# Hybrid encoder trunk on one core: down-projection steps between the last FFN products, low parts of the output weights on another engine, and a different choice of memory slots

## The chip, the cores and the metric

The kernel runs on one core of one Trainium2 chip. A core has a matrix engine (TensorE, "PE" in the profile, whose weight loads are listed as "PEld"), a vector engine (VectorE, "DVE"), a scalar engine (ScalarE, "ACT") and a general engine (GpSimd, "POOL"). Each works through its own queue in order. A fifth queue, SyncE ("SP"), issues the transfers between the chip's main memory (DRAM) and the on-chip buffers (SBUF). TensorE writes its sums into PSUM. The metric is the device time of one execution in microseconds (us). Lower is better.

## The reference

A transformer-like encoder layer is applied to two batches that share their weights: a prompt of 512 rows and a sample of 1024 rows, both 1024 wide, in 32-bit floating point. For each batch:

```python
h = rmsnorm(x); z = h @ w_in            # 1024 -> 1792, columns: q, k, v, ca, cb
a = window_attention(q, k, v)           # 8 heads of 64, |q - k| <= 128, 2 kv heads,
                                        # T5 bias, one sink logit per head
c = ca * sigmoid(cb)
c = silu(layernorm(depthwise_conv31(c)))
x = x + concat(a, c) @ w_out            # 1024 -> 1024
h = rmsnorm(x)
u = depthwise_conv3(h @ w_up)           # 1024 -> 2 * 2816
x = x + (silu(u[:, :2816]) * u[:, 2816:]) @ w_down
y = rmsnorm(x)
```

Attention looks at blocks of 128 rows and their two neighbours. The outputs are y for the prompt and y for the sample.

## The kernel before

**Products in 32 bits.** Each operand of a product is split into a high part, rounded to the format that TensorE multiplies, and a low part, the rest. A product a x b is then three matmuls into the same PSUM sums: high x high, high x low, low x high. `split` (lines 199 to 204) does it for weights: ScalarE casts the high part (L202), and VectorE or GpSimd subtracts it from the raw tile to get the low part (L203), by its argument `dve`. In the same way L969 and L965 (`split_of`) make operands of the later stages, and L1407 those of the gate columns.

**Stages.** (1) The prompt's input projection. (2) The sample's input projection (L309, L310, L312 are the three matmuls of one projection step); a side queue puts the prompt's attention, output projection and second norm between its steps (`prompt()`). (3) The prompt's FFN up projection over 22 column blocks, `ffn_step(k)`; from k = 2 on, the side queue interleaves the sample's attention and the preparation of its output weights (`sample()`). (4) The sample's output projection (L736 to L738), with sums of the prompt's gated products between. (5) The sample's FFN over 22 column blocks j, with a scheme of seven products (`first` to `seventh`, in the code's order) in place of eight per two by two blocks. Each is twelve matmuls (L1089 to L1091). (6) The down projection of both batches, by the same seven-product scheme, with the order of the products 1, 2, 5, 6, 7, 4, 3. Each has eleven steps p over pairs of column blocks; step p has three groups w, six matmuls each (L1423 to L1425): w = 0 and 1 for the sample, w = 2 for the prompt. (7) Residual, final norm and stores.

**Attention and its norm.** Scores go through VectorE (L592), ScalarE's exponential (L610), VectorE's reciprocal (L614) and a scaling (L618 on ScalarE, L620 on GpSimd). `conv_norm` transposes a block (L700), takes statistics (L702, L703), has GpSimd compute the root (L186, L187), scales (L706) and transposes back (L712). Convolution taps run on VectorE (L364), with some offloaded to ScalarE and GpSimd (L356, L357).

**The prompt's FFN step.** `up_half` runs 24 matmuls into one of two PSUM banks named u. ScalarE makes the middle tap with the bias (L866), VectorE adds two taps (L862) and so frees the bank. `gate` multiplies the two halves (L886, L891, L892).

**The sample's output weights.** In `sample()` after attention, 16 tiles of 128 x 512 are loaded (`load_wo`, L761 and L763) and split. `m % 4 < DW2` chooses VectorE for the low part; `DW2` is 0, so all 16 are on GpSimd. The prompt's 16 (`DW` = 2, `kc % 2 < DW`) are all on VectorE.

**The last FFN pair.** At j = 21, the last column block, the loop runs second, sixth, the value part of block 20, (no first of a block 22), seventh, then the first step of the down projection (two groups), (no fifth), fourth, the gate part, third. Between the sixth and the seventh lies ScalarE's copy of a sum out of PSUM (L1172), between the seventh and the fourth another (L1181). The down projection's loads come through `load_next`, which takes the next tile from a list (`ahead`): activations `ga` and gate columns `gt` or `gb` that were stored to DRAM before, and `w_down`. `operands(i, p)` makes the high and low parts for a step; `make(k + lead)` does so `lead` steps ahead of use (4 as a rule, 1 for the first step).

**What sets the order.** The program is written as one sequence. A planner simulates the engines and orders each engine's queue by readiness and by place in the program, except where `manual_schedule` keeps the written order: from the sample's FFN on for PE, and from the down projection's first step on for SP and PE. There a second block is opened after the seventh product of j = 21.

**Slots.** SBUF tiles come from a list of named slots: 15 q (4096 bytes per partition), 4 c (4224), 61 h (2048), 2 d (2176) and 32 small ones. `Slots.tile` (lines 80 to 102) takes the first free one of the smallest size that fits; freed slots go to the end of the list. A tile in a slot must wait until the last reader of the slot's former tile is done. When no slot under 4096 bytes is left, a q slot is cut into two halves of 2048 (`Half`), as long as more than `KEEP` = 3 q slots are free.

Of the kernel before, what the change touches and what calls it, by code (L numbers as in the profile page):

```python
# [15 lines left out]
P = 128  # L16
# [12 lines left out]
NJ = FF // P  # L29
# [18 lines left out]
SCB, SCD = "aapa", "aaap"  # L48


WOP, WOA, DW, DW2 = 1, 5, 2, 0
NE = 2
YN = 2
OB = "uc"
# [4 lines left out]

BACK = (200, 1500)  # L60
U0 = 2


FILL = 216
# [2 lines left out]
class Slots:  # L67
# [3 lines left out]


    def __init__(self, pool, classes, halved=None, keep=0):
        self.pool, self.free, self.n = pool, [], 0
        self.halved, self.keep, self.halves = halved, keep, {F32: [], F32R: []}
        for kind, (count, size) in classes.items():
            for i in range(count):
                self.free.append((f"{kind}{i}", size))

    def tile(self, shape, dt=F32, nbytes=4, among=None):  # L80
        need = nbytes
        for s in shape:
            need *= s
        fits = [s for s in self.free if s[1] >= need and (among is None or s[0][0] in among)]
        if self.halved and nbytes == 4 and need <= 2048 and not any(s[1] < 4096 for s in fits):
            halves = self.halves[dt]
            if not halves and sum(s[0][0] == self.halved for s in fits) > self.keep:
                slot = next(s for s in fits if s[0][0] == self.halved)
                self.free.remove(slot)
                self.n += 1  # L90
                whole = Whole(self, slot, dt, (self.pool(slot[0]) if callable(self.pool) else self.pool).tile([P, 2, 512], dt, tag=slot[0], name=f"{slot[0]}_{self.n}", bufs=1))
                halves += [(whole, 0), (whole, 1)]
                whole = None
            if halves:
                return Half(*halves.pop(0), shape)
        if not fits:
            raise RuntimeError(f"no slot for {need} bytes")
        least = min(s[1] for s in fits)
        slot = next(s for s in fits if s[1] == least)
        self.free.remove(slot)  # L100
        self.n += 1
        return Held(self, slot, (self.pool(slot[0]) if callable(self.pool) else self.pool).tile([P] + list(shape), dt, tag=slot[0], name=f"{slot[0]}_{self.n}", bufs=1))


class Held:
# [4 lines left out]
        return self.t[i]  # L110

    def __del__(self):
        self.slots.free.append(self.slot)


class Whole:
# [6 lines left out]
class Half:  # L123
# [14 lines left out]
    def __del__(self):  # L138
        w = self.whole
        w.out -= 1  # L140
        if w.out:
            w.slots.halves[w.dt].append((w, self.i))
        else:
            w.slots.halves[w.dt] = [h for h in w.slots.halves[w.dt] if h[0] is not w]
            w.slots.free.append(w.slot)


@with_exitstack
def tile_hybrid_encoder(ctx: ExitStack, tc: tile.TileContext, xs, rel_bias, norm_attn_g, w_in,
# [151 lines left out]
    def drain(queue):  # L301
        while queue:
            advance(queue)
# [531 lines left out]
    drain(side)  # L835
    load_kv()
    drain(convs)


    def want_up(k, half):  # L840
# [494 lines left out]
    def load_next(n):  # L1335
        for _ in range(n):
            if ahead:
                key, p = ahead.popleft()
                roomy = sum(f[0][0] in "qc" for f in sb.free) > 5
                if (key, p) in second_half:  # L1340
                    t = second_half.pop((key, p))
                elif key in BRIEF and p % 2 == 0 and p + 1 < NPAIR and roomy:
                    both = sb.tile([2, NT])
                    t, second_half[key, p + 1] = Part(both, 0), Part(both, 1)
                    both = None
                else:
                    t = sb.tile([NT])
                pr[key, p] = t
                what, i, n2 = key
                if what == "a":  # L1350
                    src = ga[i, p][:]
                elif what == "g":
                    n = min(2, NPAIR - 2 * p)
                    for q in range(n):
                        j, h = {1: (0, HL), 2: (1, HL), 4: (1, HR)}.get(i, (0, None))
                        src = gb[i, 2 * p + q][:] if h is None else gt[2 * (2 * p + q) + j][:, h]
                        nc.sync.dma_start(t[:, q * HT:(q + 1) * HT], src)
                    continue
                else:
                    src = w_down[0, (2 * p + i) * P:(2 * p + i + 1) * P, n2 * NT:(n2 + 1) * NT]  # L1360
                nc.sync.dma_start(t[:], src)
# [146 lines left out]
    def group(i, p, w, lead=LEAD):  # L1508

        k = ORDER.index(i) * NPAIR + p  # L1510
        if len(pr) < CAP and sum(f[0][0] == "h" for f in sb.free) > ROOM:
            load_next(1)
        make(k + lead)
        if w not in pd:
            pd[w] = wide()
        for q in range(2):
            mm_down(pd[w][:, q * NT:(q + 1) * NT], i, p, 2 * w + q)
        left[i, p] = left.get((i, p), NW3) - 1
        if left[i, p] == 0:
            hl.pop((i, p))  # L1520
            if p % 2 == 1 or p == NPAIR - 1:
                hp.pop((i, p // 2))
        if p == NPAIR - 1:
            evacuate(i, w, pd.pop(w))

    def first_step():
        load_next(8)
        for w in range(2):
            group(1, 0, w, 1)

    def product(i):
        rest = [(p, w) for p in range(2, NPAIR - 2) for w in range(NW3)]
        if i == 1:
            order = [(1, 0), (1, 1), (0, 2), (1, 2)]
        else:
            order = [(p, w) for w in range(NW3) for p in range(2)]
        order += rest + [(p, w) for w in range(NW3) for p in (NPAIR - 2, NPAIR - 1)]
        for p, w in order:
            group(i, p, w)
            if w < NW3 - 1:  # L1540
                continue
            if i == 7 and p == 4:
                load_x1(0, 0)
# [127 lines left out]
```

## Time and profile before

| What | Value |
|---|---|
| time, median of 3 runs | 1543.17 us (1542.73 to 1548.15) |
| time of the profiled execution | 1547.91 us |
| its span, from the first to the last instruction | 1546.1 us |
| TensorE busy | 1491.7 us, 96% |
| VectorE busy | 1125.0 us, 73% |
| ScalarE busy | 795.3 us, 51% |
| GpSimd busy | 704.0 us, 46% |
| moved by DMA | 227.17 MB, 147 GB/s on average |

A row of groups reads: line, engine, operation, output <- inputs by the program's names (buffer numbers left out; q, h, c, d are slots in SBUF, u, a, b, c, w banks in PSUM by the place in which they stand, other names are tensors in DRAM), shape, count, then busy us, mean ns of one, and the idle time of the engine just before them with what ended it. A row of waits reads: engine and line that waited, what it waited for, us in total, times, longest. A row of the timeline begins with the start in us and the duration. In tables of stretches each row is one stretch of the span with the busy us of each engine. Busy matmuls overlap: the profile gives one of 128x512 some 389 ns, while the next one starts earlier.

### The profile page before, as it was taken

Reading aid. Unit: us, or ns where it says so; the run is one execution under the profiler, and the core shown is the slowest. Engines: PE = TensorE matmul, PEld = TensorE weight load, DVE = VectorE, ACT = ScalarE, POOL = GpSimd, SP = SyncE. Lnnn points to the kernel's source line nnn. Section 1 sums busy time; section 2 is a strip of 40 time slices with the busy share of each in tenths; the row PEclk is TensorE's granted clock in tenths of the full one; section 3 lists DMA queues with packets and bytes.
Section 4 is the critical chain, followed back from the end, with each engine's and each line's share of the span. In section 5 each row is a group of like instructions: output and inputs, shape, how many; then the busy total and the mean of one; then the engine's idle time right before and its main releaser. Section 6 shows DMA issues by size and latency. Waiting matters only on the chain.

```text
span 1546.1 us, 20081 instructions
## 1 busy us (share of the span) xinstructions
PE 1491.7 (96%) x6843; PEld 1228.5 (79%) x6843; DVE 1125.0 (73%) x1608; ACT 795.3 (51%) x1404; POOL 704.0 (46%) x562
## 2 busy tenths in 40 slices
PE   8999998899999999899999999999999899999998
PEld 6787787787888888777777888888888788888886
DVE  7998767857879795434677777777776855668885
ACT  4644654335777776713454544555445633343355
POOL 7652343225667766956423555555545000003345
PEclk9999999899999999999999999999999999999999
DMA  6572334447344435868422233333331582356654
GB/s 226 163 216 80 104 102 125 130 132 223 103 130 130 131 121 165 257 215 287 158 82 69 96 107 105 102 103 102 103 133 51 194 299 86 108 166 214 211 184 163
DMA packets 228780, 227.17 MB, mean 147 GB/s; under 512 B 13268, under 2 KB 168348, under 8 KB 228549
## 3 DMA queue, kind: packets, MB, share of 16 engines
q1 hardware_dynamic: 228677, 225.88, 45.4%
q8 instruction: 54, 0.88, 0.2%
q14 instruction: 49, 0.40, 0.1%
HBM read 164.74 MB, written 62.14 MB: 147 GB/s over the span
## 4 chain that ended last, share of the span: by engine, by line
PE 72%; DMA 4%; DVE 2%; POOL 2%; ACT 2%; issue 1%; SPq 1%; POOLq 0%; ACTq 0%; DVEq 0%
PE w L1091 8%; PE w L1090 8%; PE w L1089 8%; PE w L1423 7%; PE w L1424 7%; PE w L1425 7%; PE u L312 5%; PE u L309 5%; PE u L310 5%; PE u L736 1%; PE u L738 1%; PE u L737 1%; DMA h<-gt 1%; PE b L309 1%; PE b L310 1%
## 5 line engine op out<-in xcount | busy, mean ns | idle before, releaser
L203 POOL TENSOR_TENSOR q<-q,q 128x1024 fp32r<-128x1024 f32 x72 | 173.5, 2415 | 93.6 <-ACT q L202 37.6
L965 POOL TENSOR_TENSOR q<-q,q 128x512 fp32r<-128x512 f32 x101 | 140.7, 1399 | 157.9 <-ACT q L1075 145.8
L965 DVE TENSOR_TENSOR h<-h,h 128x512 fp32r<-128x512 f32 (+2 forms) x202 | 158.2, 816 | 63.1 <-ACT h L969 24.3
L1423 PE MATMUL w<-h,h 128*128 128x512 f32 x462 | 179.8, 389 | 0.6 <-ACT h L969 0.6
L1425 PE MATMUL w<-h,h 128*128 128x512 f32 x462 | 179.8, 389 | 0.0
L1424 PE MATMUL w<-h,h 128*128 128x512 f32 x462 | 179.7, 389 | 0.0
L1089 PE MATMUL w<-h,q 128*128 128x512 f32 x448 | 175.1, 391 | 3.9 <-ACT w L1181 2.2
L1091 PE MATMUL w<-h,q 128*128 128x512 f32 x448 | 174.5, 389 | 1.1 <-POOL q L965 1.1
L309 PE MATMUL u<-h,q 128*128 128x512 f32 x400 | 160.0, 400 | 7.7 <-DVE h L862 4.6
L1090 PE MATMUL w<-h,q 128*128 128x512 f32 x426 | 165.8, 389 | 0.0
L310 PE MATMUL u<-h,q 128*128 128x512 f32 x400 | 157.9, 395 | 0.0
L312 PE MATMUL u<-h,q 128*128 128x512 f32 x384 | 152.4, 397 | 1.3 <-POOL q L203 1.3
L364 DVE SCALAR_TENSOR_TENSOR c<-c,cvw,c 128x512 f32<-128x512 f32 x184 | 138.0, 750 | 2.9
L962 POOL TENSOR_TENSOR q<-q,q 128x1024 f32<-128x1024 f32 x12 | 32.8, 2742 | 235.6 <-DMA h<-gb 195.5
L969 ACT CAST h<-h 128x512 fp32r<-128x512 f32 x120 | 71.7, 620 | 96.7 <-DVE h L965 47.7
L309 PE MATMUL b<-h,q 128*128 128x512 f32 x256 | 102.8, 401 | 4.0 <-DVE d L394 2.9
L1089 PEld LDWEIGHTS w<-h,q 128*128 128x128 f32 x448 | 84.1, 188 | 22.5 <-ACT w L1181 2.6
L862 DVE SCALAR_TENSOR_TENSOR h<-u,fw,h 128x511 f32<-128x511 f32 x88 | 65.4, 743 | 50.3 <-ACT h L866 49.5
L1423 PEld LDWEIGHTS w<-h,h 128*128 128x128 f32 x462 | 86.7, 188 | 19.1 <-ACT h L969 1.0
L310 PE MATMUL b<-h,q 128*128 128x512 f32 x256 | 101.5, 396 | 0.0
L312 PE MATMUL b<-h,q 128*128 128x512 f32 x256 | 101.5, 396 | 0.0
L1425 PEld LDWEIGHTS w<-h,h 128*128 128x128 f32 x462 | 86.7, 188 | 18.1
(417 smaller groups left out, 3656.1 us busy)
## 6 DMA issues: line engine op xcount, KB each, us to landing
q<-in_w_up SPq DMA_DIRECT2D x88, 512.0 KB
ga<-q SPq DMA_DIRECT2D x64, 256.0 KB
h<-ga SPq DMA_DIRECT2D x57, 256.0 KB
q<-in_w_in SPq DMA_DIRECT2D x28, 512.0 KB
h<-in_w_down SPq DMA_DIRECT2D x52, 256.0 KB
q<-in_x_sample SPq DMA_DIRECT2D x15, 512.0 KB
h<-qsd SPq DMA_DIRECT2D x24, 256.0 KB
x1d<-q SPq DMA_DIRECT2D x11, 512.0 KB
```

Source lines behind the costliest of these rows:

```text
L203: (nc.vector if dve else nc.gpsimd).tensor_tensor(lo[:], raw[:], hi[:].bitcast(F32), op=ALU.subtract)
L309: nc.tensor.matmul(out, whi[:, kc, :], hi[:], start=(kc == 0), stop=False)
L310: nc.tensor.matmul(out, whi[:, kc, :], lo[:], start=False, stop=False)
L312: nc.tensor.matmul(out, wlo[:, kc, :], hi[:], start=False, stop=(kc == KC - 1))
L364: nc.vector.scalar_tensor_tensor(acc[:], src(t), w(t), acc[:], op0=ALU.mult, op1=ALU.add)
L965: (eng or nc.vector).tensor_tensor(out, a, b, op=ALU.subtract)
L1089: nc.tensor.matmul(out, whi[:, s], hi[:], start=(start and c == 0), stop=False, **go)
L1090: nc.tensor.matmul(out, whi[:, s], lo[:], start=False, stop=False, **go)
L1091: nc.tensor.matmul(out, wlo[:, s], hi[:], start=False, stop=(stop and c == 3), **go)
L1423: nc.tensor.matmul(out, sh[:, c], th[:], start=(p == 0), stop=False)
L1424: nc.tensor.matmul(out, sh[:, c], tl[:], start=False, stop=False)
L1425: nc.tensor.matmul(out, sl[:, c], th[:], start=False, stop=(p == NPAIR - 1))
```

## The change

Three things are changed.

1. In the last FFN pair (j = 21), the second block of hand-written order for SP and PE is opened before the seventh product instead of after it, and 18 tiles are loaded there in one go (before: 10 and then 8). Four steps p = 0 to 3 of the down projection's first product, with their groups w = 0 and 1, are put between the pair's products: two groups before the seventh, two between the seventh and the fourth, two between the fourth and the third, and two after the third. Before, two groups of step 0 stood there. Their operands are made one step ahead. `product(1)` then leaves out the groups already done.
2. `DW2` is 4 instead of 0: the low parts of all 16 tiles of the sample's output weights are subtracted on VectorE instead of GpSimd.
3. `Slots.tile` counts its calls as a clock and notes when each slot and each half became free. A free half is taken in place of a whole small slot when it has been free longer than the first small slot that fits. While `sb.old` is `OLD` = 24 (from the side queue's `prompt()` to the end of the sample's input projection), a q slot is also cut into halves when the small slot on offer has been free for fewer than 24 calls and the q slot for longer, if more than `KEEP` q slots are free. Otherwise `sb.old` is 0 and a q slot is cut only when no small slot fits, as before.

```diff
-WOP, WOA, DW, DW2 = 1, 5, 2, 0
+WOP, WOA, DW, DW2 = 1, 5, 2, 4
+OLD = 24
...
+    def give(self, slot):
+        self.since[slot[0]] = self.clock
+        self.free.append(slot)
+
+    def split_whole(self, slot, dt):
+        self.free.remove(slot)
+        self.n += 1
+        t = (...).tile([P, 2, 512], dt, tag=slot[0], name=f"{slot[0]}_{self.n}", bufs=1)
+        whole = Whole(self, slot, dt, t)
+        since = self.since.get(slot[0], -OLD)
+        self.halves[dt] += [(whole, 0, since), (whole, 1, since)]
+
     def tile(self, shape, dt=F32, nbytes=4, among=None):
+        self.clock += 1
...
-        if self.halved and nbytes == 4 and need <= 2048 and not any(s[1] < 4096 for s in fits):
+        least = min((s[1] for s in fits), default=0)
+        slot = next((s for s in fits if s[1] == least), None)
+        if self.halved and nbytes == 4 and need <= 2048:
             halves = self.halves[dt]
-            if not halves and sum(s[0][0] == self.halved for s in fits) > self.keep:
...
-            if halves:
-                return Half(*halves.pop(0), shape)
+            wholes = [s for s in fits if s[0][0] == self.halved]
+            since = self.since.get(slot[0], -OLD) if slot and slot[1] < 4096 else self.clock
+            if halves and (min(h[2] for h in halves) < since or since == self.clock):
+                return Half(*self.oldest(halves), shape)
+            if (since == self.clock or self.clock - since < self.old) and len(wholes) > self.keep and \
+                    self.since.get(wholes[0][0], -OLD) < since:
+                self.split_whole(wholes[0], dt)
+                return Half(*self.oldest(halves), shape)
...
     side.append(prompt())
+    sb.old = OLD
     pace.update(rate=RB, conv=CB, late=CL)
...
     drain(convs)
+    sb.old = 0
...
-    def first_step():
-        load_next(8)
-        for w in range(2):
-            group(1, 0, w, 1)
+    filled = set()
+
+    def fill(*which):
+        for p, w in which:
+            group(1, p, w, 1)
+            filled.add((p, w))
 
     def product(i):
         rest = [(p, w) for p in range(2, NPAIR - 2) for w in range(NW3)]
+        order = [(p, w) for w in range(NW3) for p in range(2)]
+        order += rest + [(p, w) for w in range(NW3) for p in (NPAIR - 2, NPAIR - 1)]
         if i == 1:
-            order = [(1, 0), (1, 1), (0, 2), (1, 2)]
-        else:
-            order = [(p, w) for w in range(NW3) for p in range(2)]
-        order += rest + [(p, w) for w in range(NW3) for p in (NPAIR - 2, NPAIR - 1)]
+            order = [g for g in order if g not in filled]
...
         value_part(j - 1)
+        last = j == NJ - 1
+        if last:
+            by_hand.__exit__(None, None, None)
+            by_hand = tc.manual_schedule(engines={mybir.EngineType.SP, mybir.EngineType.PE})
+            by_hand.__enter__()
+            load_next(18)
+            fill((0, 0), (1, 0))
         first(j + 1)
         split_up(j + 1, 6)
         seventh(j)
-        if j == NJ - 1:
-            by_hand.__exit__(None, None, None)
-            by_hand = tc.manual_schedule(engines={mybir.EngineType.SP, mybir.EngineType.PE})
-            by_hand.__enter__()
-            load_next(10)
-            first_step()
+        if last:
+            fill((0, 1), (1, 1))
         fifth(j + 1)
         split_up(j + 1, 7)
         fourth(j)
         gate_part(j)
         split_up(j + 1, 4)
+        if last:
+            fill((2, 0), (2, 1))
         third(j)
         split_up(j + 1, 3)
+    fill((3, 0), (3, 1))
```

More of the change, by code (lines that the diff above doesn't have):

```diff
@@ L73, in __init__ @@
     def __init__(self, pool, classes, halved=None, keep=0):
-        self.pool, self.free, self.n = pool, [], 0
+        self.pool, self.free, self.n, self.clock, self.since, self.old = pool, [], 0, 0, {}, 0
         self.halved, self.keep, self.halves = halved, keep, {F32: [], F32R: []}
@@ L78, in __init__ @@
                 self.free.append((f"{kind}{i}", size))
+    def give(self, slot):
[4 more added lines that the diff above has]
+        self.n += 1
+        t = (self.pool(slot[0]) if callable(self.pool) else self.pool).tile([P, 2, 512], dt, tag=slot[0], name=f"{slot[0]}_{self.n}", bufs=1)
+        whole = Whole(self, slot, dt, t)
+        since = self.since.get(slot[0], -OLD)
+        self.halves[dt] += [(whole, 0, since), (whole, 1, since)]
     def tile(self, shape, dt=F32, nbytes=4, among=None):
+        self.clock += 1
         need = nbytes
@@ L84, in tile @@
         fits = [s for s in self.free if s[1] >= need and (among is None or s[0][0] in among)]
-        if self.halved and nbytes == 4 and need <= 2048 and not any(s[1] < 4096 for s in fits):
+        least = min((s[1] for s in fits), default=0)
+        slot = next((s for s in fits if s[1] == least), None)
+        if self.halved and nbytes == 4 and need <= 2048:
             halves = self.halves[dt]
-            if not halves and sum(s[0][0] == self.halved for s in fits) > self.keep:
[L88 to L93, printed above, removed]
-            if halves:
-                return Half(*halves.pop(0), shape)
-        if not fits:
+            wholes = [s for s in fits if s[0][0] == self.halved]
[6 more added lines that the diff above has]
+                return Half(*self.oldest(halves), shape)
+        if slot is None:
             raise RuntimeError(f"no slot for {need} bytes")
-        least = min(s[1] for s in fits)
-        slot = next(s for s in fits if s[1] == least)
         self.free.remove(slot)
@@ L102, in tile, with oldest @@
         return Held(self, slot, (self.pool(slot[0]) if callable(self.pool) else self.pool).tile([P] + list(shape), dt, tag=slot[0], name=f"{slot[0]}_{self.n}", bufs=1))
+    @staticmethod
+    def oldest(halves):
+        h = min(halves, key=lambda h: h[2])
+        halves.remove(h)
+        return h[0], h[1]
 class Held:
@@ L112, in __del__ @@
     def __del__(self):
-        self.slots.free.append(self.slot)
+        self.slots.give(self.slot)
 class Whole:
@@ L141, in __del__ @@
         if w.out:
-            w.slots.halves[w.dt].append((w, self.i))
+            w.slots.halves[w.dt].append((w, self.i, w.slots.clock))
         else:
-            w.slots.halves[w.dt] = [h for h in w.slots.halves[w.dt] if h[0] is not w]
-            w.slots.free.append(w.slot)
+            w.slots.halves[w.dt][:] = [h for h in w.slots.halves[w.dt] if h[0] is not w]
+            w.slots.give(w.slot)
 @with_exitstack
```

## The prediction

> **What bounds the kernel.** I read the page first, then TensorE's waits over the whole run, then tables of stretches around each wait. The page's head and the row of busy time:
>
> ```profile
> span 1546.1 us, 20081 instructions
> ...
> PE 1491.7 (96%) x6843; PEld 1228.5 (79%) x6843; DVE 1125.0 (73%) x1608; ACT 795.3 (51%) x1404; POOL 704.0 (46%) x562
> ```
>
> TensorE is busy 96% of the span. The change removes no matmul, so all it can win is in the 1546.1 - 1491.7 = 54.4 us when TensorE stands idle, and in matmuls at a reduced clock. Where these lie, from TensorE's list of waits (releaser: us in total, times, longest):
>
> ```profile
> PE u L309 <- DVE h L862: 4.6, 2, 3.5
> PE u L712 <- DVE q L706: 4.0, 1, 4.0
> PE u L712 <- DVE h L706: 3.4, 1, 3.4
> ...
> PE u L312 <- POOL q L203: 1.3, 3, 0.6
> ```
>
> No wait is longer than 4.0 us and each has its own place. Three tables of stretches give the stages that the change touches (columns: stretch, length, then PE, PEld, DVE, ACT, POOL busy us with instruction counts, granted clock, DMA share, GB/s):
>
> ```profile
> 245.00:285.00 40.00, 30.87 (x133) 24.50 (x132) 25.82 (x41) 19.84 (x37) 18.48 (x15) 0.87 0.51 151
> ...
> sum 285.00, PE 266.59 PEld 217.77 DVE 213.32 ACT 136.73 POOL 106.28; mean PE 44.43 PEld 36.30 DVE 35.55 ACT 22.79 POOL 17.71
> ...
> 276.00:282.00 6.00, 5.19 (x14) 4.01 (x14) 3.29 (x6) 4.68 (x11) 2.56 (x2) 0.53 0.52 178
> ...
> 640.00:651.00 11.00, 11.00 (x50) 9.10 (x49) 2.34 (x4) 8.11 (x13) 10.92 (x8) 1.00 0.85 290
> 651.00:668.00 17.00, 12.35 (x47) 9.42 (x46) 5.74 (x8) 4.47 (x8) 15.74 (x11) 0.90 0.59 180
> ...
> 1212.00:1232.00 20.00, 15.93 (x68) 12.19 (x67) 18.70 (x27) 12.55 (x22) 0.00 (x0) 1.00 0.67 228
> 1232.00:1243.00 11.00, 11.00 (x50) 9.12 (x49) 9.95 (x13) 2.76 (x5) 0.00 (x0) 1.00 0.28 107
> ```
>
> The sum row covers 105 to 390 us, the prompt's attention under the sample's projection: TensorE is idle 285.0 - 266.6 = 18.4 us there. After a long stall the clock is low for some us as well: 6 us at 0.53 after the two waits on L706, which costs 0.47 x 6 = 2.8 us, and 0.90 over 17 us after the 3.5 us wait on L862, 1.7 us. After the waits of 1.3 and 2.2 us at 1212 it stays 1.00. The last row gives the pace: 50 matmuls in 11 us, 0.22 us each, so a down-projection group of six is 1.3 us and a product of twelve 2.6 us.
>
> **Part 1, the last FFN pair.** Today one group stands between the sixth and the seventh product and one between the seventh and the fourth; none between the fourth and the third. From the timeline:
>
> ```profile
> 1212.78 0.68 DVE L965 TENSOR_TENSOR h<-q,h 128x512 fp32r<-128x512 f32 x1
> ...
> 1214.60 0.50 PE L1089 MATMUL w<-h,q 128*128 128x512 f32 x1 [1.29 <-ACT h L1172]
> ...
> 1215.71 1.28 DVE L965 TENSOR_TENSOR h<-h,h 128x512 fp32r<-128x512 f32 x2
> ...
> 1217.94 0.62 ACT L969 CAST h<-h 128x512 fp32r<-128x512 f32 x1 [3.40 <-DMA h<-in_w_down]
> ...
> 1218.12 1.21 DVE L1229 TENSOR_TENSOR q<-q,q 128x1024 f32<-128x1024 f32 x1
> ...
> 1221.18 0.50 PE L1089 MATMUL w<-h,q 128*128 128x512 f32 x1 [2.16 <-ACT w L1181]
> ...
> 1226.24 0.32 SPq L1361 DMA_DIRECT2D h<-ga  x1
> ...
> 1230.27 0.47 PE L1423 MATMUL w<-h,h 128*128 128x512 f32 x1 [0.62 <-ACT h L969]
> ```
>
> The three waits are 1.29 + 2.16 + 0.62 = 4.07 us. Each is a copy or cast on ScalarE, stuck behind casts of down-projection operands. The changed order puts two groups (2.6 us) in each of the first two gaps and two more pairs after the fourth and the third. **First gap:** the second group, of pair 1, moves 1.3 us of work in front of the seventh product, as long as the wait. But it needs the low parts of pair 1 from VectorE, and in today's order these come at 1213.5 (the L965 row that reads q) and in the two at 1215.71, the first of which ends at 1216.4. If VectorE keeps that order, the group starts at 1216.5 in place of 1213.2, and everything in the strict order behind it with it: the seventh product would begin 3.3 us later than now, with 1.3 us more work done, so 2.0 us are lost there. **Second gap:** the copy L1181 is late because ScalarE stood 3.40 us on a w_down load; the loads now stand ahead of the seventh product. They fill 18 tiles in 21 transfers (three gate tiles take two each), at the 0.32 us of the SP row 6.7 us of issue. What they pass on SP is nothing of the seventh product's, which moves no data; the last of them fetches the product of block 20, which VectorE finishes at 1219.3 (L1229) and which today goes out at 1226.24. SP therefore still stands at that one, and behind it wait only tiles that the sixth group and later ones use. **Third:** pairs 2 and 3 are needed some 5 and 10 us after pair 1, and the four remaining groups of the third column pair (5.3 us) follow before pair 4. No matmul is added. VectorE is the engine without room, 18.70 of 20 us with the same work after as before; it is late next. Bounds: all three waits, -4.1; and with the 2.0 us lost in the first gap but 2.16 + 0.62 won behind it, -0.8. I take **-3.5**, near the full gain: pair 1's low parts now stand ahead of the seventh product in the program, so the planner has cause to put them first.
>
> **Part 2, sixteen low parts of the output weights.** The prices, from the instructions of L203 (POOL from 600 to 670, VectorE from 100 to 390, the latter being the same subtraction in the prompt's weights) and the groups from 600 to 670:
>
> ```profile
> L203 POOL TENSOR_TENSOR h<-h,h x16: 1275/1291/1318, 629.9 to 665.5; 128x512 fp32r<-128x512 f32 x16
> L203 POOL TENSOR_TENSOR q<-q,q x10: 2351/2400/2422, 604.1 to 655.7; 128x1024 fp32r<-128x1024 f32 x10
> ...
> L203 DVE TENSOR_TENSOR h<-h,h x12: 675/691/693, 222.3 to 319.9; 128x512 fp32r<-128x512 f32 x12
> L203 DVE TENSOR_TENSOR q<-h,h x4: 691/933/1447, 288.7 to 322.6; 128x512 fp32r<-128x512 f32 x4
> ...
> L862 DVE SCALAR_TENSOR_TENSOR h<-u,fw,h 128x511 f32<-128x511 f32 x18 | 13.5, 748 | 27.8 <-ACT h L866 27.6
> ```
>
> POOL loses 16 x 1.291 = 20.7 us, VectorE gains 16 x 0.691 = 11.1 us, in a stretch where POOL is full (10.92 of 11, 15.74 of 17) and VectorE is not (2.34 and 5.74). What POOL also does there is the low parts of the up weights at 2.4 us, on which the FFN's third matmul (L312) waits. The timeline shows what follows from the full queue:
>
> ```profile
> 651.11 7.00 POOL L203 TENSOR_TENSOR q<-q,q 128x1024 fp32r<-128x1024 f32 x3
> ...
> 652.85 0.40 PE L310 MATMUL u<-h,q 128*128 128x512 f32 x1
> ...
> 656.74 0.47 PE L309 MATMUL u<-h,q 128*128 128x512 f32 x1 [3.50 <-DVE h L862]
> ...
> 665.04 0.39 PE L312 MATMUL u<-h,q 128*128 128x512 f32 x1
> ```
>
> A projection starts its first two matmuls, and its third, which needs the low part, stands in TensorE's order behind a whole other projection; that one has no bank yet and waits 3.5 us. If the low part came 5 us sooner, the started projection (24 x 0.22 = 5.3 us) would cover that wait. But the bank's own chain is not POOL's:
>
> ```profile
> 649.53 3.14 DMA h<-in_w_out
> ...
> 653.22 0.59 ACT b L886
> 653.81 0.54 ACT h L202
> 654.35 0.69 ACT h L866
> 655.06 0.76 DVE h L862
> ```
>
> A late w_out load holds the cast on ScalarE, the casts hold the bias pass L866, that holds the taps L862 which free the bank. The casts stay on ScalarE, so this chain stays. Bounds: the 3.5 us wait with its 1.7 us of low clock, -5.2; and against it VectorE work ahead of the taps. A bank turns in 0.69 + 2 x 0.75 = 2.2 us against 5.3 us of matmuls in the other bank, 3.1 us to spare; four low parts (2.8 us) in front of one tap are free, seven together, as POOL runs them now at 658, cost 7 x 0.69 - 3.1 = 1.7 us, and stretched to the longest row, 1.447, 7.0 us, with 1.7 us of low clock 8.7. I take **-3.5**, the wait alone.
>
> The Trainium skill, SBUF — State Buffer, section "SBUF: two separate sides", has a rule against this move: a VectorE operation with two inputs in SBUF and a GpSimd one that reads SBUF take one port pair in turn, and the loser stands still for the whole instruction. By it a low part could last 0.69 plus the rest of a POOL subtraction. The row of four with 1447 ns as its longest may be that; the twelve at 675 to 693 show nothing of it.
>
> **Part 3, which slot a tile gets.** It adds and removes no instruction and no byte, and its comparison of ages holds outside attention too; it changes which earlier reader a new tile waits for, and through it the planner's order of every engine but the parts written by hand. Waits for a slot are those for the reader of the tile before, such as a store. From POOL's and SP's lists of waits in the stretch 105 to 370, and ScalarE's group of projection casts from 105 to 285:
>
> ```profile
> POOL q L203 <- DMA qsd<-q: 11.0, 1, 11.0
> ...
> SPq L196 <- PE a L641: 16.6, 1, 16.6
> ...
> L202 ACT CAST q<-q 128x1024 fp32r<-128x1024 f32 x10 | 10.5, 1048 | 8.7 <-DMA vsd<-q 4.2 <-POOL q L203 2.6 <-PE b L312 1.8
> ```
>
> They stand on POOL, SP and ScalarE, while TensorE's long waits there (L706, 4.0 and 3.4 us) end in a chain of arithmetic: norm, POOL's root, scaling. A freer slot doesn't shorten these. Bounds: all 18.4 idle us and the 2.8 us of clock won, -21; or one stall of the size of the two on L706 more, +7.4 + 2.8 = +10. The nearest TensorE rows to a slot are the waits on POOL's weights, 1.3 us over the run. I take **-2.0**.
>
> **The sum.** -3.5 - 3.5 - 2.0 = -9.0 us against the profiled execution's own 1547.91 us (span 1546.1) is 1538.9. That execution is 4.7 us above the median of the runs shown (1543.17), so I set the forecast at 1543.17 - 9.0 = 1534.2, say **1534 us**.
>
> **Rivals.** (A) Only part 1 pays: the chain through ScalarE's casts keeps its 3.5 us, and the slots only rename waits. 1543.2 - 3.5 = **1540**. For it: the chain above and the arithmetic behind L706. Against it: POOL's queue is full exactly where the low part is missed. (B) The low parts crowd the taps, stretched as in the 1447 ns row: +8.7 - 3.5 = +5.2, **1548**. For it: a bunch of seven stands on POOL today; VectorE's queue is in order, and behind a low part that waits for a cast stand the taps, the gate and the attention's maxima. Against it: the VectorE rows with 27.8 us of idle time, and casts that already come before L866. The rule of the Trainium skill above would bring this case about. (C) The slower one: whole slots run short. The new rule cuts a 4 KB slot in two under attention when small slots are fresh; each projection chunk needs three whole ones (raw, high, low). A load issued late exposes transfer, cast and low part. SP already stands 16.6 us for such a slot (L196), and TensorE has 2 chunks x 48 x 0.22 = 21 us in hand. With an estimated 3.5 us of transfer (0.52 MB at the 151 GB/s of the first stretch), 1.05 of cast and 2.4 of low part, 7.0 us, it decides from a load some 14 us later than now. Each such chunk that comes 5 us late costs 5 + 2.8 (clock) = 7.8 us; two: 15.6 - 3.5 = +12.1, **1555**. For it: three whole slots are kept back, as many as one chunk needs. Against it: TensorE waits only 1.3 us on L203 in the whole run.
>
> **Numbers.** Forecast 0.46 (its own range 1526 to 1538), A 0.28, B 0.12, C 0.14. The range leaves out C and a little of the largest slot gains: **1524 to 1548**. About 0.5%, 7.7 us, is what a measurement of this kernel can tell from no change, so faster means under 1535.5, slower above 1550.9. Of the forecast's 0.46 some 0.40 lies below 1535.5, and A adds 0.07 where the slots pay more: faster 0.47; C makes slower 0.14; the rest is 0.39.
>
> **What would show it.** Part 1: in TensorE's waits the rows on L1172, L1181 and L969 near 1215 us gone; wrong if a group there waits on ScalarE or VectorE. Part 2: L203 on POOL without its sixteen, no stretch with POOL at 0.9, the wait on L862 under 1 us; wrong (B) if waits on L862 grow or the new VectorE L203 rows lie near 1.4 us. Part 3: idle time from 105 to 390 near 16 us; wrong (C) if TensorE waits on L203 or L202 of w_in. The forecast falls if the waits on L706 grow.

## The result, and the profile after

The changed kernel takes 1536.95 us, median of 8 runs (1530.34 to 1538.92), against 1542.57 us (1540.00 to 1548.15, 8 runs) before. The ratio is 0.9944, with a 95% interval of 0.9927 to 0.9962, that is 8.6 us less (5.9 to 11.3). It is not the quotient of the two medians, which lie 5.6 us apart (0.9964); the runs of each kernel spread over some 8 us. The forecast was 1534 us and faster; the range of 1524 to 1548 holds the time, and the median lies 1.5 us above the 1535.5 us under which the prediction spoke of faster. The profiled execution took 1537.94 us. Its page begins:

```profile
span 1536.2 us, 20069 instructions
...
PE 1491.5 (97%) x6843; PEld 1229.2 (80%) x6843; DVE 1151.5 (75%) x1624; ACT 795.7 (52%) x1404; POOL 694.5 (45%) x546
```

TensorE does the same 6843 matmuls in the same busy time; its idle time fell from 54.4 to 1536.2 - 1491.5 = 44.7 us. Part of that is chance of the execution: the profiled one before took 1547.91 us, 5.3 us above the median of its kernel. Sixteen instructions have gone from POOL to VectorE. VectorE's busy time rose by 26.5 us where 11.1 were worked out: some of its instructions last longer now. Line numbers are 20 to 22 higher than before (L203 is now L223, L862 is L884, L965 is L987, L1089 is L1111); the kernels with only part 1 or only part 2 keep the old ones.

**The last FFN pair.** TensorE's list of waits between 1190 and 1240 us has one row left of the three, and it is a new one:

```profile
PE w L1445 <- DVE q L1232: 1.3, 1, 1.3
```

The timeline there shows why the first two are gone, and what the third has become:

```profile
1203.34 0.68 DVE L987 TENSOR_TENSOR h<-q,h 128x512 fp32r<-128x512 f32 x1
1203.94 1.28 DVE L987 TENSOR_TENSOR h<-h,h 128x512 fp32r<-128x512 f32 x2
...
1206.61 0.39 PE L1445 MATMUL w<-h,h 128*128 128x512 f32 x1
...
1206.93 0.58 ACT L1194 COPY h<-w 128x512 f32<-128x512 f32 x1
...
1207.54 1.22 DVE L1249 SCALAR_TENSOR_TENSOR q<-q,q 128x1024 f32<-128x1024 f32 x1
...
1224.37 1.27 DVE L1232 SCALAR_TENSOR_TENSOR q<-w,fw,q 128x1023 f32<-128x1023 f32 x1
...
1225.79 0.47 PE L1445 MATMUL w<-h,h 128*128 128x512 f32 x1 [1.34 <-DVE q L1232]
```

Pair 1's low parts (among the L987 rows at 1203.34 and 1203.94) now stand well ahead of block 20's value part (L1249) on VectorE; before, by the prediction's reading, the last of them came at 1215.71, behind it. So the second group ran from 1206.61 without a wait, and ScalarE's copy out of PSUM (L1194) was finished under it. What is left is a bank: the first group of the third column pair needs the one that the last gate part's taps (L1232) free, and VectorE is late with these.

**The prompt's last FFN steps.** TensorE's waits from 595 to 770 us, first rows:

```profile
PE u L329 <- DVE h L884: 4.0, 1, 4.0
PE a L720 <- DMA h<-cvd: 2.1, 1, 2.1
PE c L758 <- DMA h<-catd: 1.5, 1, 1.5
```

The wait on the taps, which part 2 was to remove, is still there, 4.0 us where it was 3.5 and 1.2. The chain that ended last shows another cause than before:

```profile
646.73 2.77 DVE h L223
...
650.26 0.69 DVE h L223
...
650.99 0.76 DVE h L884
```

Then it was a w_out load and ScalarE's casts; now it is the low parts (L223) on VectorE, ahead of the taps. They are also far longer than 0.69 us. Rows of L223 on VectorE from 633 to 652 us, then from 654 to 661, then on POOL from 633 to 652, then the taps, and the attention's low parts that read PSUM (L664), from 600 to 665 (min/median/max in ns):

```profile
L223 DVE TENSOR_TENSOR h<-h,h x7: 682/2851/3752, 633.6 to 650.3; 128x512 fp32r<-128x512 f32 x7
...
L223 DVE TENSOR_TENSOR h<-h,h x5: 682/693/693, 655.4 to 659.4; 128x512 fp32r<-128x512 f32 x5
...
L223 POOL TENSOR_TENSOR q<-q,q x4: 2392/2792/2825, 634.4 to 646.1; 128x1024 fp32r<-128x1024 f32 x4
...
L884 DVE SCALAR_TENSOR_TENSOR h<-u,fw,h x16: 733/749/752, 605.0 to 661.6; 128x511 f32<-128x511 f32 x16
...
L664 DVE TENSOR_TENSOR h<-a,h x5: 673/677/680, 605.7 to 633.0; 128x512 fp32r<-128x512 f32 x5
```

Beside one of POOL's 128x1024 subtractions, VectorE's subtraction of two SBUF tiles lasts 2.85 us or more (four of the seven) instead of 0.69, and POOL's own has a median of 2.79 instead of 2.40. The two engines go by turns, four instructions against four (L914 is a product of the FFN step):

```profile
638.97 1.61 POOL L914 TENSOR_TENSOR h<-h,h 128x512 f32<-128x512 f32 x1 [2.14 <-DVE h L884]
...
639.35 10.16 DVE L223 TENSOR_TENSOR h<-h,h 128x512 fp32r<-128x512 f32 x4
...
640.63 8.33 POOL L223 TENSOR_TENSOR q<-q,q 128x1024 fp32r<-128x1024 f32 x3
```

As soon as POOL has none left, it is 0.69 again. VectorE's work with one operand in PSUM (L884, L664) keeps its time throughout, beside POOL's subtractions too. The taking of turns is what the Trainium skill, SBUF — State Buffer, section "SBUF: two separate sides", says of a VectorE operation with two SBUF inputs beside a GpSimd one that reads SBUF: one of them stands still until the other has finished. The trace agrees, with 2.85 us for 0.69.

**The attention.** The sum of the same stretches from 105 to 390 us:

```profile
sum 285.00, PE 272.59 PEld 223.84 DVE 224.00 ACT 143.51 POOL 108.80; mean PE 45.43 PEld 37.31 DVE 37.33 ACT 23.92 POOL 18.13
```

TensorE is idle 12.4 us there, after 18.4. Single executions differ here: the kernels with only part 1 or only part 2, whose order up to 600 us is that of the kernel before, show 15.9 and 16.9 us. The two waits on the scaling in the norm (L706, now L726, 4.0 and 3.4 us) are not among its waits in this stretch any more. The longest is now that of a score matmul on VectorE's convolution taps, which was 1.6 us before:

```profile
PE a L605 <- DVE c L384: 4.2, 1, 4.2
```

### The profile page after: what moved, and what is told of

It reads as the page before. It is cut to its first block, busy times and chain, and to the rows that moved or that the text cites. A ratio compares the mean times of both kernels' runs of the same rounds, so it can differ in the third digit from the quotient of the medians.

```text
span 1536.2 us, 20069 instructions
## 1 busy us (share of the span) xinstructions
PE 1491.5 (97%) x6843; PEld 1229.2 (80%) x6843; DVE 1151.5 (75%) x1624; ACT 795.7 (52%) x1404; POOL 694.5 (45%) x546
## 4 chain that ended last, share of the span: by engine, by line
PE 49%; DMA 3%; POOL 2%; DVE 1%; ACT 1%; issue 1%; SPq 1%; POOLq 0%; ACTq 0%; DVEq 0%
PE w L1113 8%; PE w L1111 8%; PE w L1112 8%; PE w L1445 7%; PE w L1446 7%; PE w L1447 7%; DMA h<-gt 1%; POOL h L926 0%; PE u L329 0%; PE u L756 0%; PE u L330 0%; PE u L332 0%; PE u L758 0%; PE u L757 0%; DMA gt<-h 0%
## 5 line engine op out<-in xcount | busy, mean ns | idle before, releaser
L223 POOL TENSOR_TENSOR q<-q,q 128x1024 fp32r<-128x1024 f32 x72 | 175.1, 2437 | 115.6 <-ACT q L222 43.5
L987 POOL TENSOR_TENSOR q<-q,q 128x512 fp32r<-128x512 f32 x101 | 140.4, 1397 | 153.5 <-ACT q L1097 141.4
L987 DVE TENSOR_TENSOR h<-h,h 128x512 fp32r<-128x512 f32 (+2 forms) x202 | 154.0, 795 | 65.5 <-ACT h L991 25.5
L1111 PE MATMUL w<-h,q 128*128 128x512 f32 x448 | 174.8, 390 | 0.4 <-ACT w L1185 0.4
L1445 PEld LDWEIGHTS w<-h,h 128*128 128x128 f32 x458 | 86.0, 188 | 19.7 <-issue 1.7
L1447 PEld LDWEIGHTS w<-h,h 128*128 128x128 f32 x462 | 86.7, 188 | 17.9
L222 ACT CAST q<-q 128x1024 fp32r<-128x1024 f32 (+1 forms) x73 | 75.9, 1044 | 47.5 <-POOL q L223 16.9
L1446 PEld LDWEIGHTS w<-h,h 128*128 128x128 f32 x458 | 86.0, 188 | 17.7
```

The costliest lines, as they stand in the source:

```text
L223: (nc.vector if dve else nc.gpsimd).tensor_tensor(lo[:], raw[:], hi[:].bitcast(F32), op=ALU.subtract)
L987: (eng or nc.vector).tensor_tensor(out, a, b, op=ALU.subtract)
L1111: nc.tensor.matmul(out, whi[:, s], hi[:], start=(start and c == 0), stop=False, **go)
L1445: nc.tensor.matmul(out, sh[:, c], th[:], start=(p == 0), stop=False)
L1446: nc.tensor.matmul(out, sh[:, c], tl[:], start=False, stop=False)
L1447: nc.tensor.matmul(out, sl[:, c], th[:], start=False, stop=(p == NPAIR - 1))
```

## The experiments

Each kernel was timed beside runs of the kernel before on the same chip; the ratios are to those runs, with 95% intervals. One per cent is 15.4 us.

**Each part alone, and all but the one that looked harmful.** Two theories: P, that part 1 and the slots make the gain and part 2 none; Q, that the trace shows a reshuffle (or, of part 2, that it is needed).

Only part 1. Edit: `fill`, the loads and the order of `product(1)` as in the change, nothing else.

> Only part 1 (the four steps between the last products) is put into the kernel before; everything ahead of the sample's FFN is then the same program as before. Theory P (the whole change's gain is made of part 1 and of the slots): TensorE's lost time between 1200 and 1250 us falls from 5.0 to about 1.6 us, nothing else moves, ratio about 0.998 (-3.4 us). Theory Q (what the trace of the whole change shows is a reshuffle in which no part has a price of its own): other stretches move too, ratio anywhere from 0.993 to 1.003.

Measured: 0.9976 (0.9963 to 0.9989), 3.7 us less (1.7 to 5.7), as predicted. In the last pair one wait of 1.1 us was left of 4.1. It is the first of the three, which the second group was to cover:

```profile
1207.78 0.62 ACT L1407 CAST h<-h 128x512 fp32r<-128x512 f32 x1 [1.68 <-DMA h<-gt]
...
1209.97 0.50 PE L1089 MATMUL w<-h,q 128*128 128x512 f32 x1 [1.11 <-ACT h L1172]
```

Here ScalarE stood 1.68 us on a gate tile, and the copy came behind the casts that followed. In the changed kernel it came ahead of them.

Only part 2. Edit:

```diff
-WOP, WOA, DW, DW2 = 1, 5, 2, 0
+WOP, WOA, DW, DW2 = 1, 5, 2, 4
```

> Only part 2 (the 16 low parts of the sample's output weights on VectorE). The prediction priced it at -3.5 us: the wait of TensorE on the taps near 655 us (3.5 us) gone, ratio 0.9975. Theory P after the trace of the whole change: VectorE's low parts beside POOL's 128x1024 subtractions last over 2 us each, stand ahead of the taps and bring a wait of 3 to 5 us of the same kind in place of the one removed; ratio 0.999 to 1.003. Theory Q: the wait is gone, 0.997 to 0.998.

Measured: 1.0027 (1.0012 to 1.0041), 4.2 us more (1.9 to 6.3). The prediction's step for part 2 falls; the ratio lies in P's range. TensorE's first row of waits from 595 to 770 us, and L203 on VectorE from 600 to 670:

```profile
PE u L309 <- DVE h L862: 5.3, 2, 4.0
...
L203 DVE TENSOR_TENSOR h<-h,h x16: 677/691/3155, 625.6 to 665.4; 128x512 fp32r<-128x512 f32 x16
```

Without the other parts too, the wait on the taps is no shorter (4.6 us before), and single low parts last up to 3.2 us. The wait grew by 0.7 us only; where the rest of the 4.2 us is lost, the trace does not show.

Only part 3. Edit: the class `Slots`, `Half`, `OLD` and the two settings of `sb.old`.

> Only part 3 (which slot a tile gets). Theory P: the attention stretch 105 to 390 us loses about 7 us less than before (idle 18.4 us to about 12), ratio 0.995 to 0.996. Theory Q (the gain there needs the others, or is chance of the order): ratio 0.998 to 1.003, idle time there 16 to 20 us.

Measured: 0.9984 (0.9967 to 1.0002), 2.5 us less, not clear of nothing. Its profile has the attention's gain, and a last pair (old order of the groups) that waits more than before on the bank of the third group:

```profile
sum 285.00, PE 275.03 PEld 225.92 DVE 225.99 ACT 143.90 POOL 110.12; mean PE 45.84 PEld 37.65 DVE 37.66 ACT 23.98 POOL 18.35
...
PE w L1445 <- ACT q L1230: 3.9, 1, 3.9
```

Idle time from 105 to 390 us is 10.0 us, as P expected. The profiled execution is the shortest of this kernel's runs (1537.73 us; they go up to 1548.83), so the ratio counts here and not the span.

Parts 1 and 3 without part 2. Edit: `DW2` back to 0 in the changed kernel.

> The changed kernel with the 16 low parts of part 2 back on GpSimd (parts 1 and 3 kept). Theory P: nothing is lost, ratio to before 0.992 to 0.995, at or below the changed kernel's 0.9944. Theory Q (part 2 relieves POOL): the wait of 3.5 us with its 1.7 us of low clock returns on top of what the changed kernel has, ratio 0.997 to 0.998.

Measured: 0.9940 (0.9925 to 0.9956). The whole gain is there without part 2; the changed kernel's 0.9944 is not to be told from it. Part 3 on top of part 1 takes 0.9976 to 0.9940, 5.6 us, more than the 2.5 alone, though the intervals leave open whether it is more. The wait on the taps is 4.7 us in this kernel, and its chain is the old one, from a store through a w_out load to ScalarE's casts:

```profile
637.95 4.24 DMA catd<-h
...
642.26 3.14 DMA h<-in_w_out
...
645.95 0.59 ACT b L908
646.54 0.54 ACT h L222
647.08 0.69 ACT h L888
```

So part 2 replaced a wait of this size by one of the same size with another cause.

**Which rule of part 3, and how large.** Theory S: tiles in freshly freed slots under attention are what costs, and cutting a q slot avoids it. Theory H: the order of the halves does it. Theory R: it is a chance of the planner's order. Base: parts 1 and 3 (0.9940). Edits, one each:

```diff
-    sb.old = OLD
+    sb.old = 0
...
-OLD = 24
+OLD = 12
...
-OLD = 24
+OLD = 48
...
-OLD = 24
+OLD = 96
```

> Parts 1 and 3 without part 2, and sb.old left at 0: only the rule that an older half goes before a younger small slot is left of part 3; no whole slot is cut while small ones are free. Base is the kernel with parts 1 and 3 (0.994). Theory S (fresh slots under attention are what costs): the idle time from 105 to 390 us goes back to near 18 us, ratio 0.9965 to 0.998, that is part 1 alone. Theory H (the order of halves, or merely another order, does it): 0.993 to 0.995 as the base.

> Parts 1 and 3 without part 2, with OLD = 12 in place of 24 (a whole slot is cut only where the small slot on offer has been free for fewer than 12 allocations). Theory S: between no cut (0.997) and the base (0.994), since the freshest slots are avoided still; about 0.995. Theory R (the gain is a chance of the planner's order): unrelated to the size of OLD, anywhere from 0.991 to 1.001.

> Parts 1 and 3 without part 2, with OLD = 48 in place of 24. Theory S: at least the base's gain, 0.992 to 0.9945, unless whole slots run short, which would show as TensorE waits on the weights' low parts (L223 of the projection) and SP waits for whole slots. Theory R: anywhere from 0.991 to 1.001.

> Parts 1 and 3 with OLD = 96. Theory S (a whole slot cut early saves waits for fresh small ones): 0.991 to 0.993 as with 48, unless whole slots run short: then SP waits longer for whole slots of w_in (L216) than with 48 and the idle time from 105 to 390 us rises above 12 us, ratio above 0.994.

Measured, in the same order (no cut, 12, 48, 96): 1.0076 (1.0058 to 1.0094), 0.9938 (0.9917 to 0.9959), 0.9921 (0.9902 to 0.9941), 0.9929 (0.9917 to 0.9942). Below is the stretch from 105 to 390 us of part 1 alone, no cut, 12, the base with 24, 48 and 96. The number of matmuls done stands in brackets behind TensorE's busy time; the third number from the end is the granted clock.

```profile
105.00:390.00 285.00, 269.15 (x1248) 220.35 (x1247) 216.85 (x387) 139.39 (x282) 107.29 (x81) 0.98 0.44 132
...
105.00:390.00 285.00, 262.58 (x1198) 213.31 (x1198) 204.99 (x359) 135.09 (x268) 101.64 (x78) 0.96 0.43 128
...
105.00:390.00 285.00, 269.83 (x1264) 221.88 (x1263) 219.10 (x402) 143.68 (x289) 107.71 (x81) 0.99 0.45 135
...
105.00:390.00 285.00, 274.16 (x1265) 224.84 (x1264) 224.26 (x401) 143.60 (x289) 108.14 (x80) 0.97 0.45 135
...
105.00:390.00 285.00, 274.28 (x1286) 226.10 (x1285) 228.32 (x408) 143.87 (x292) 109.67 (x83) 0.98 0.47 137
...
105.00:390.00 285.00, 275.31 (x1293) 227.75 (x1293) 230.10 (x411) 145.24 (x296) 111.69 (x83) 0.98 0.47 139
```

TensorE's idle time there (285.0 less its busy time) is 15.9 us with part 1 alone, then 22.4, 15.2, 10.8, 10.7 and 9.7. H falls: with the order of the halves alone the kernel is 0.8% slower than before. That is worse than S expected, too: taking an old half in place of a small slot, with no slot cut for it, costs by itself some 15 us against part 1 alone. In the two traces the kernels are 17.8 us apart (spans of 1554.5 and 1536.7 us). By 390 us the kernel without cuts is 50 matmuls behind, some 11 us at the 0.22 us each of the prediction (an estimate): it has 6.5 us more idle time and a lower clock, 0.96 for 0.98. Where the other 7 us lie was not followed.

That cutting is worth some 21 us against not cutting (0.9940 for 1.0076) holds for this kernel. How much the threshold matters is less clear. 48 and 96 give the same program: their traces hold the same instructions in the same order on every engine, so 0.9921 and 0.9929 are one kernel measured twice. 12 has the ratio and the matmuls of 24, with the idle time of part 1 alone at a higher clock. The intervals of 12, 24 and 48 overlap, so R is not excluded among them; and that the gain comes from avoided waits for fresh slots, as S says, was not followed from wait to wait. Whole slots do not run short: SP's waits for the whole slots of w_in in this stretch come to 33 us in the changed kernel and 53 with 48, against 55 before. So the slower rival C has no sign here.

**Are the low parts slow by their number, or by the other engine?** Theory L: the engines exclude each other. Theory C: VectorE has too many operations. Edit, on the whole change, which gives VectorE eight more subtractions and leaves POOL none beside its sixteen:

```diff
-            upw[k, half] = split(upr.pop((k, half)))
+            upw[k, half] = split(upr.pop((k, half)), k >= 18)
```

> The whole change, and in the last four FFN blocks of the prompt (k = 18 to 21) the low parts of the up weights (eight of 128x1024) on VectorE too, so that GpSimd no longer subtracts beside VectorE's 16 low parts of the output weights. VectorE gets some 8 x 1.22 = 9.8 us more work. Theory L (the two engines exclude each other, and each of VectorE's subtractions waits out GpSimd's): the L223 128x512 rows on VectorE fall from up to 3.75 us to 0.69 each, the wait on the taps (4.0 us) shrinks to under 2 us, ratio to before 0.991 to 0.994. Theory C (VectorE is crowded by the number of operations): the wait on the taps grows to 6 us or more, ratio 0.996 to 1.000.

Measured: 0.9933 (0.9914 to 0.9952). L223 on VectorE from 590 to 665 us, and TensorE's first row of waits from 595 to 770:

```profile
L223 DVE TENSOR_TENSOR h<-h,h x16: 676/689/1540, 624.4 to 657.6; 128x512 fp32r<-128x512 f32 x16
...
L223 DVE TENSOR_TENSOR q<-q,q x8: 1214/1220/2322, 612.3 to 644.9; 128x1024 fp32r<-128x1024 f32 x8
...
PE c L758 <- DMA h<-catd: 4.3, 1, 4.3
```

With half as many operations again on VectorE, the sixteen are back at a median of 0.69 us and the wait on the taps is gone from the list. The longest, 1.54 us, ran beside a product that GpSimd keeps (L914). L holds, C falls. But the time is the changed kernel's within the intervals: the next thing to be late is the load of the attention's result, and it waits 4.3 us in place of the 4.0.

**Versions built on what was learnt.** All have OLD = 48. First, two groups of step 4 behind the last product, for the bank wait:

```diff
-    fill((3, 0), (3, 1))
+    fill((3, 0), (3, 1), (4, 0), (4, 1))
```

> Parts 1 and 3 with OLD = 48 (0.992) and two more groups, of step 4, between the last product and the first group of the third column pair. Theory B (the last wait, 1.3 to 2.1 us on the taps of the last gate part, is for a PSUM bank, and 2.7 us of other matmuls cover it): the wait on L1232 near 1225 us gone, ratio lower by 0.001. Theory V (VectorE has no room there): operands of step 4 come earlier in its queue, the taps later, the wait stays at 1.3 us or more or turns into one for step 4's operands; ratio unchanged.

Measured: 0.9931 (0.9915 to 0.9946). TensorE has no wait left between 1190 and 1245 us, as B expected, against V; but the ratio is not lower than without (0.9921). A gain of two microseconds is less than these intervals can show.

Second, output weights loaded earlier, for the chain through ScalarE's casts (parts 1 and 3):

```diff
-WOP, WOA, DW, DW2 = 1, 5, 2, 0
+WOP, WOA, DW, DW2 = 1, 8, 2, 0
```

> Parts 1 and 3 with OLD = 48, and the sample's output weights loaded eight tiles ahead of their split in place of five (WOA = 8). Theory D (the wait of 3 to 3.5 us on the taps near 650 us comes from the late w_out load, which holds ScalarE's cast and the bias pass behind it): the wait on L884 halves at least, ratio lower by 0.001 to 0.003. Against it: the three more raw tiles take small slots, loads wait for slots instead, and nothing is won.

Measured: 0.9929 (0.9915 to 0.9943). The wait on L884 near 650 us is what it was. The first row is the kernel with WOA = 5, the others are with 8:

```profile
644.61 0.47 PE L329 MATMUL u<-h,q 128*128 128x512 f32 x1 [2.99 <-DVE h L884]
...
641.78 0.61 PE L329 MATMUL u<-h,q 128*128 128x512 f32 x1 [2.93 <-DVE h L884]
...
638.75 1.44 ACT L888 ACTIVATE h<-u,vecs,fw 128x512 f32<-128x512 f32 x2 [1.29 <-DMA gt<-h]
```

Over the whole run the waits on L884 fell from 5.0 us (three) to this one, but the two that went were small, and one of them stood at 371 us, long before the output weights. ScalarE's bias pass (L888) now waits for a store. So D's forecast fails: with the weights loaded earlier another release comes last, the wait is as long, and the ratio did not fall.

Third, the whole change with the up weights' last low parts on VectorE, as above:

> The whole change with OLD = 48 and the up weights' low parts of k = 18 to 21 on VectorE, so that no GpSimd subtraction stands beside the 16 low parts. If the parts' prices add: 0.992 less the 0.001 that the move of the up weights' low parts gave against the changed kernel, 0.990 to 0.992. If not, the stretch 600 to 660 us is decided by the transfers (w_out, cat) and not by the low parts at all: 0.991 to 0.994, with TensorE's waits there on transfers.

Measured: 0.9903 (0.9890 to 0.9916), a median of 1528.38 us against 1544.40: the fastest of all, ahead of the kernel before (by 15.0 us by the ratio) and of the changed kernel. Its number is that of prices which add; but its longest wait from 595 to 770 us, 3.5 us, is on a transfer (L758 on catd), the sign of the other theory. That part 2 is worth having once POOL does not subtract beside it is likely but not shown: 0.9903 here against 0.9921 without part 2 and this move, and the two intervals overlap. L223 from 590 to 665 us:

```profile
L223 DVE TENSOR_TENSOR h<-h,h x16: 676/690/933, 615.8 to 647.4; 128x512 fp32r<-128x512 f32 x16
```

## Why the prediction was right, and where it was not

**The sum** was -9.0 us against a measured -8.6. That they agree is luck: part 2 gave +0.6 on top of the others in place of -3.5, and part 3 -5.6 beside part 1 in place of -2.0.

**Part 1, -3.5: right in size**, -3.7 measured alone. The argument that decided it, that the planner would put pair 1's low parts in front, is seen in the timeline (1203.34 and 1203.94, ahead of L1249). The warning that VectorE is late next was right as well: the remaining 1.3 us is its taps. By the prediction's own sign (a group there waits on VectorE) that is a miss of this size. Alone, the part left the first wait nearly whole (1.1 us of 1.3), because ScalarE stood on a gate tile there. What I did not name is that the third column pair's first group waits for a PSUM bank: the four groups that the prediction counted as cover are the ones that wait.

**Part 2, -3.5: wrong in sign**, +4.2 alone and nothing that can be told (+0.6) on top of the other parts. The failed step is the duration: "VectorE gains 16 x 0.691 = 11.1 us" was taken from the prompt's rows, and "the twelve at 675 to 693 show nothing of it" misread them. In that trace none of the twelve has a GpSimd instruction beside it. Of the other four, two have one, and these are the long ones. VectorE's and GpSimd's rows there:

```profile
288.72 1.17 DVE L203 TENSOR_TENSOR q<-h,h 128x512 fp32r<-128x512 f32 x1
...
291.26 1.45 DVE L203 TENSOR_TENSOR q<-h,h 128x512 fp32r<-128x512 f32 x1
...
288.04 1.30 POOL L667 TENSOR_TENSOR q<-q,h 64x512 fp32r<-64x512 f32 x1 [7.84 <-DVE q L665]
289.50 2.65 POOL L203 TENSOR_TENSOR q<-q,q 128x1024 fp32r<-128x1024 f32 x1 [0.17 <-ACT q L202]
```

So the kernel before already showed what would happen. Beside POOL's 128x1024 subtractions the low parts then lasted 2.85 to 3.75 us. Rival B had this mechanism, with the longest row as its price; its place (ahead of the taps) is confirmed by the chain, and its price for one instruction was low. The rule of the Trainium skill (SBUF — State Buffer, section "SBUF: two separate sides") that was weighed against the move spoke for B, and the run with the neighbouring subtractions taken from POOL shows that these cause the long durations. In the changed kernel the mechanism cost little that can be seen, a wait of 4.0 us where 4.7 us stand without part 2; but the intervals of the two kernels leave room for a loss of some 4 us, as alone. The wait does not account for that loss, which stays open.

**Part 3, -2.0: right in sign, too small.** It gave -2.5 alone, with an interval that reaches zero, and -5.6 beside part 1. The step "a freer slot doesn't shorten these", said of the two waits on L706, failed: both are gone in the changed kernel, and stand at 4.0 and 2.9 us in the kernels with part 1 or part 2 alone. The arithmetic chain did not get shorter: from the first transpose of such a block to the first one back it took 4.6 and 4.0 us before (265.51 to 270.14, 270.64 to 274.60), and takes 10.7 and 8.2 us now (252.53 to 263.19, 282.80 to 291.01). What changed is that TensorE has other matmuls ready all the while. I priced the slots by the waits that name a slot, and not by the order that they allow. If the part gains more beside part 1, one cause is seen: with the new slots and the old order the last pair waits 3.9 us on its bank, of which the fills leave 1.3.

**Rivals.** A (only part 1 pays, 1540) is refuted by the run without part 2. B came half true, as said. C, the slower one, did not happen in any run: the slots were cut and whole ones did not run short, up to OLD = 48 (96 gave the same program).

## What to carry to other kernels

Before work is moved from GpSimd to VectorE, look at what GpSimd goes on doing beside it: a subtraction of two SBUF tiles cost 0.69 us alone and 2.85 us beside a 128x1024 one on GpSimd, and the move stood in the fastest kernel only with that one gone as well. When a row's duration is taken from another stage, see what ran beside it there. Where a hand-written order leaves an engine waiting for a copy out of PSUM, independent groups that are worth the length of the wait remove it, if their operands are put ahead in the other engines' queues and the copy does not stand behind a late load. The choice of buffers changes the planned order far from any wait that names a buffer, so time it whole, and vary its threshold: here the cutting rule gave 21 us against its own absence.

## What the runs showed of the hardware

VectorE and GpSimd held each other up in whole instructions, not by a share: 682 to 693 ns with GpSimd quiet, 2.85 us and more beside GpSimd's 128x1024 subtractions, and no change (673 to 752 ns) for VectorE work with one operand in PSUM. The size had not been expected. One VectorE instruction can stand through two of GpSimd's: the longest, 3752 ns from 633.63, began beside one (633.19 to 634.48) and ended 0.55 us after the next (634.44 to 636.83). Executions of one program differ by some 8 us, before and after the change, as much as the whole gain. In the changed kernel the granted clock goes with it, 0.992 in the shortest of the eight (1530.34 us) and 0.988 in the longest (1538.92); what sets it was not tried.
